# A two-layer hybrid SSM backbone on one core: layer 0's normed input leaves PSUM on two engines, S5 tables are computed without a wait for memory, and the order of background steps changes

## The chip, the cores and the metric

The kernel runs on one core of a Trainium2 chip. Its engines are TensorE (PE, matrix products into PSUM), VectorE (DVE), ScalarE (ACT), GpSimd (POOL) and SyncE (SP, which here only issues transfers). Each engine runs its own list of instructions in order, and instructions of different engines are tied by semaphores. The metric is the device time of one execution in microseconds (us); lower is better.

## The reference, cut to what matters

Two layers work on 512 tokens, 256 of context and 256 latent, of 1024 values each. A conditioning vector gives six modulation rows per layer through a matrix-vector product (`w_mod`); rows 0 and 1 shift and scale the normed input of the mixer, row 2 gates the mixer's result, rows 3 to 5 do the same around the feed-forward block.

```python
def _modulate(h, shift, scale):
    return h * (1.0 + scale) + shift
...
    for l in range(DEPTH):
        m_l = jnp.split((s_c @ w_mod[l] + b_mod[l])[:, None, :], N_MOD, axis=-1)
        m_c = jnp.split(s_cc @ w_mod[l] + b_mod[l], N_MOD, axis=-1)
        p_l = _split_in(_modulate(_rms_norm(x, norm_mix[l]), m_l[0], m_l[1]) @ w_in[l])
        p_c = _split_in(_modulate(_rms_norm(ctx, norm_mix[l]), m_c[0], m_c[1]) @ w_in[l])
        ...  # S5, retention and gated linear attention on columns of p_c and p_l
        x = x + m_l[2] * _merge_branches((s5_l, ret_l, gla_l), p_l[11:14], w_brs, w_out[l])
        x = x + m_l[5] * _swiglu(_modulate(_rms_norm(x, norm_ffn[l]), m_l[3], m_l[4]), w_ffn_in[l], w_ffn_out[l])
```

The S5 branch needs tables that hang on its parameters alone: powers and rotations of 64 complex states, made of exponentials, sines and cosines. They do not depend on the tokens.

## The kernel before, in words

**Products.** All large products are fp32 split in two rounded parts: an operand is hi + lo, and a product is three matmuls, hi·hi, hi·lo and lo·hi (`mm3`). SP loads a weight tile into a ring of three (`raw`), ACT rounds it (`hi`, line 228), DVE subtracts (`lo`, line 231; both in a ring of four). Tokens lie in the buffer `rb`, hi and lo beside each other, with the 1024 features on 8 blocks of 128 partitions.

**Order.** A list scheduler with a simulated timeline and priorities (`prio`) fixes, at build time, the order of each engine's instructions; on the chip each engine takes them strictly in that order. Memory in SBUF is handed out by two allocators, `arena` (20992 words per partition) and `zone` (5632 words). A new object takes the piece that was freed longest ago, and its first writer waits for whoever used that piece last. PSUM has rings of four banks (`mm`, accumulators), three (`mx`) and one (`sd`).

**The head of layer 0.** `layer` (line 1315 on) loads the tokens and scales them by their inverse norm (`xscale`, results `xs`). Then it goes over four chunks c of 256 features:

- `mod_chunk(c)` makes shift and scale of these features: two transfers of 1 MB (line 437), a matrix-vector product of 64 small matmuls and 8 for the bias, one row copy by ACT, one transpose, three small DVE steps into `mod`. In the page and the trace this is `b<-arena,sil`, `arena<-b 128x128` and `mod<-b`.
- `norm_chunk(c)` transposes the chunk, 8 blocks of 128 by 128 in two banks. DVE multiplies each bank by the scale (`arena<-b,mod` 128x512, line 231) and adds the shift (`arena<-arena,mod`), which gives one fp32 object of 1024 per partition (`h32`). ACT rounds all of it into `rb` hi (128x1024), DVE subtracts into `rb` lo (128x1024).
- `pack_mms(c)` runs 24 matmuls 128x512 into four accumulators, with weights from `pack_weights` (lines 540 and 541).

`pack_out` then empties the four accumulators, and `load_params2` transposes further parameters.

**S5 tables and asides.** `s5_tables` computes the tables in `zone`; `hold`, an object of 1536 words in `zone`, is given back only after it. Other work that hangs on no token is kept as a list of generators, the asides; later stages call `tick`, which runs the next step of the first. They are the two S5 rotations (`s5_rot`), the S5 preparations (`s5_prep`) and the modulation rows that the head does not make (`mod_vec`, rows 2 to 5 of layer 0 and 0 to 5 of layer 1). Rows listed in `ON_VECTOR`, among them 4 and 5 of layer 0, are accumulated by DVE: per 128 rows of weights one step of 128x1024 for each of two accumulators (`zone<-wm,sil,zone`), 16 in all; rows 2 to 5 of layer 1 have one accumulator, 8 steps. The bias row of each is loaded by SP into `zone`.

**Around the asides** stand layer 0's mixers, gates (up to about 405 us), merge (the branch projections and their sum, about 405 to 455 us), the output product and the feed-forward block (FFN).

## Time and profile before

| | |
|---|---|
| three runs | 1400.59, 1400.7 and 1404.64 us, median 1400.7 us |
| profiled execution, first to last instruction (span) | 1395.2 us; its own time is not given beside it, and the median is 5.5 us above the span |
| mean granted TensorE clock | 0.985 |
| busy: PE, DVE, ACT, POOL | 1344.3, 908.3, 577.4 and 75.6 us |
| moved by DMA | 257.33 MB, 184 GB/s on average |

A busy time is the sum over an engine's instructions. A wait is the time in which an engine has nothing to run, put down to the instruction or transfer whose semaphore came last. A window gives for a stretch of the span each engine's busy time, the granted TensorE clock as a share of full speed, and what the transfers moved. The list of the head's instructions by time runs from 0 to about 65 us, where the last matmul of chunk 3 ends.

### The profile page before, as it was taken

What the parts mean: (1) busy time and instruction counts of PE and PEld (TensorE: products, weight loads), DVE (VectorE), ACT (ScalarE), POOL (GpSimd) and SP (SyncE); (2) the same over time, 40 slices, a digit from 0 to 9 for tenths busy, and PEclk for the clock granted to TensorE, in tenths of its full rate; (3) what the DMA queues carried; (4) which work ended last, traced back from release to release, by engine and by line L of the source; (5) the groups of instructions that cost most, each with busy time, mean ns of one, the idle gap of its engine ahead of it and who ended that gap; (6) DMA issues with size and microseconds to landing.
All of it is one profiled execution on the core that took longest, in us unless ns stands there. A gap on an engine that the chain in (4) does not pass through costs nothing.

```text
span 1395.2 us, 22070 instructions
## 1 busy us (share of the span) xinstructions
PE 1344.3 (96%) x8559; PEld 1140.9 (82%) x8559; DVE 908.3 (65%) x1423; ACT 577.4 (41%) x930; POOL 75.6 (5%) x111
## 2 busy tenths in 40 slices
PE   4899999999999999999999999999999999899996
PEld 3788888787777778788777778888999997899985
DVE  4579782838889564545554788645876778555555
ACT  3367352323432343222222447545564364444442
POOL 3310000001100020000000000100000100000000
PEclk9999999999999999999999999999999999899999
DMA  9744465668968554733344786644766866466662
GB/s 305 213 115 119 139 200 182 213 197 271 303 210 280 173 165 125 234 109 121 106 129 129 279 310 193 181 112 111 199 170 163 238 191 215 117 198 197 184 192 91
DMA packets 258817, 257.33 MB, mean 184 GB/s; under 512 B 27200, under 2 KB 219244, under 8 KB 258200
## 3 DMA queue, kind: packets, MB, share of 16 engines
q1 hardware_dynamic: 244360, 230.41, 55.0%
q10 hardware_dynamic: 11392, 20.39, 4.2%
q0 software_dynamic: 2960, 5.12, 1.4%
q8 instruction: 67, 1.10, 0.3%
q14 instruction: 38, 0.31, 0.1%
HBM read 231.79 MB, written 24.08 MB: 183 GB/s over the span
## 4 chain that ended last, share of the span: by engine, by line
PE 85%; DMA 6%; DVE 5%; issue 2%; ACT 2%; SPq 1%; DVEq 0%; POOL 0%; POOLq 0%; ACTq 0%
PE b L243 83%; PE b L253 2%; DVE arena L231 2%; DVE lo L231 1%; DMA wm<-in_w_mod_dram 1%; DMA arena<-in_w_mod_dram 1%; DMA raw<-in_w_in_dram 1%; DMA raw<-in_w_ffn_out_dram 1%; DMA arena<-wb 1%; ACT arena L228 1%; DMA arena<-in_ctx_dram 1%; ACT hi L228 1%; DVE rb L231 0%; DVE zone L234 0%; DMA raw<-in_w_ffn_in_dram 0%
## 5 line engine op out<-in xcount | busy, mean ns | idle before, releaser
L243 PE MATMUL b<-rb,hi 128*128 128x256 f32 (+1 forms) x2784 | 695.1, 340 | 6.2 <-ACT rb L228 4.7
L243 PEld LDWEIGHTS b<-rb,hi 128*128 128x128 f32 x2784 | 481.9, 193 | 70.1 <-issue 11.1
L228 ACT ACTIVATE hi<-raw 128x1024 fp32r<-128x1024 f32 (+3 forms) x298 | 293.0, 989 | 458.0 <-PE b L243 350.4
L243 PE MATMUL b<-rb,lo 128*128 128x256 f32 (+1 forms) x1392 | 471.3, 339 | 0.0
L231 DVE TENSOR_TENSOR lo<-raw,hi 128x1024 fp32r<-128x1024 f32 (+3 forms) x298 | 338.3, 1140 | 199.4 <-ACT hi L228 190.4
L243 PE MATMUL b<-hi,rb 128*128 128x512 f32 (+2 forms) x1168 | 346.2, 374 | 3.9 <-DVE arena L570 3.3
L243 PEld LDWEIGHTS b<-rb,lo 128*128 128x128 f32 x1392 | 268.7, 193 | 31.7 <-issue 5.4
L243 PEld LDWEIGHTS b<-hi,rb 128*128 128x128 f32 x1168 | 216.5, 188 | 39.2 <-issue 4.1
L243 PE MATMUL b<-lo,rb 128*128 128x512 f32 (+2 forms) x584 | 217.0, 373 | 0.0
L243 PE MATMUL b<-arena 64*64 64x96 f32 (+8 forms) x1104 | 132.8, 288 | 0.3 <-DVE arena L231 0.3
L243 PEld LDWEIGHTS b<-lo,rb 128*128 128x128 f32 x584 | 109.8, 188 | 15.3 <-issue 1.3
L243 PEld LDWEIGHTS b<-arena 128*128 128x128 f32 (+4 forms) x1104 | 102.6, 167 | 20.2 <-issue 7.1
L231 DVE TENSOR_TENSOR arena<-arena 128x512 f32<-128x512 f32 (+5 forms) x174 | 105.6, 622 | 17.7 <-ACT arena L228 16.7
L234 DVE SCALAR_TENSOR_TENSOR arena<-arena,b 128x512 f32<-128x512 f32 (+1 forms) x136 | 74.2, 552 | 51.0 <-PE b L243 50.6
L228 ACT ACTIVATE arena<-b 128x512 f32<-128x512 f32 (+6 forms) x138 | 66.5, 486 | 73.9 <-PE b L243 59.6
L228 ACT ACTIVATE rb<-arena 128x256 fp32r<-128x256 f32 (+3 forms) x133 | 60.8, 473 | 84.3 <-PE b L243 57.2
L231 DVE TENSOR_TENSOR zone<-zone 128x512 f32<-128x512 f32 (+6 forms) x127 | 73.7, 604 | 28.6 <-DMA wb<-zone 17.4
L234 DVE SCALAR_TENSOR_TENSOR zone<-wm,sil,zone 128x1024 f32<-128x1024 f32 x56 | 70.9, 1283 | 18.7 <-DMA wm<-in_w_mod_dram 18.3
L231 DVE TENSOR_TENSOR rb<-arena,rb 128x256 fp32r<-128x256 f32 (+2 forms) x106 | 54.4, 522 | 21.1 <-ACT rb L228 20.7
L228 ACT ACTIVATE arena<-arena 128x512 f32<-128x512 f32 (+3 forms) x61 | 36.5, 601 | 30.6 <-DVE arena L231 19.9
L253 PE MATMUL b<-cst,arena 128*128 128x128 f32 (+1 forms) x178 | 30.4, 290 | 18.8 <-DMA arena<-in_norm_mix_dram 9.6
L491 POOL TENSOR_TENSOR st<-st,mh 128x1 f32<-128x1 f32 x16 | 11.6, 727 | 658.9 <-DVE st L240 657.9
(137 smaller groups left out, 660.4 us busy)
## 6 DMA issues: line engine op xcount, KB each, us to landing
raw<-in_w_ffn_in_dram SPq DMA_DIRECT2D x88, 512.0 KB
wm<-in_w_mod_dram SPq DMA_DIRECT2D x80, 512.0 KB
raw<-in_w_ffn_out_dram SPq DMA_DIRECT2D x66, 512.0 KB
raw<-in_w_in_dram SPq DMA_DIRECT2D x48, 512.0 KB
raw<-in_w_in_dram SPq DMA_DIRECT2D x48, 384.0 KB
raw<-in_w_out_dram SPq DMA_DIRECT2D x16, 512.0 KB
arena<-in_w_mod_dram SPq DMA_DIRECT2D x7, 1024.0 KB
wb<-zone ACTq DMA_DIRECT2D x8, 512.0 KB
```

Of the source, the lines that this page charges most:

```text
L228: self.S.activation(out, in_, f, bias=bias, scale=scale)
L231: self.V.tensor_tensor(out=out, in0=a, in1=b, op=op)
L234: self.V.scalar_tensor_tensor(out=out, in0=a, scalar=s, in1=b, op0=op0, op1=op1)
L243: self.P.matmul(out, l, r, start=start, stop=stop, **k)
L253: self.P.transpose(out, in_, self.ident[:k, :k])
L491: self.G.tensor_tensor(out=st[:, 3:4], in0=st[:, 2:3], in1=self.mh[:, 0:1], op=ALU.pow)
```

## The change

`norm_chunk` works on half a bank at a time: ACT computes scale times value plus shift straight from PSUM and writes the rounded result into `rb` (four ACT steps of 128x256 per chunk in place of one of 128x1024). DVE computes the same from PSUM in full precision with one two-operation step (`tensor_scalar`, four of 128x256 per chunk in place of two products and two sums of 128x512), and subtracts per bank (two of 128x512 in place of one of 128x1024). The transposes in a bank are ordered by feature block. In the kernel after, an ACT step and a DVE step that read the same bank are ordered one behind the other by semaphores.

All weights of `mod_chunk` and all four `xs` lie in `arena`, `hold` is gone, so `zone` is empty when `s5_tables` is built. The rotation of layer 0 follows at once and is no aside; the rotation of layer 1 stands in the list right ahead of layer 1's preparation. The list of modulation rows was 2 3 4 5 of layer 0, then 2 1 0 3, layer 1's preparation, 4 5 of layer 1. It is now 2 3 4 of layer 0, 1 0 of layer 1, 5 of layer 0, 2 3 of layer 1, rotation and preparation, 4 5 of layer 1.

```diff
 def asides(self, names):
     for c in names:
         if c == "p":
+            self.aside("rot", self.s5_rot(1, self.s5d[1]))
             self.aside("prep1", self.s5_prep(1, self.s5d[1]))
...
     for m in (1, 0):
-        ws[m] = (self.zone if c == 3 and m else self.arena).new(KD, 256)
+        ws[m] = self.new(KD, 256)
...
 def norm_chunk(self, c, xs):
     ks = slice(2 * c, 2 * c + 2)
-    h32 = self.new(4, 2, 128)
+    sh, sc = self.mod[:, 0, 0], self.mod[:, 0, 1]
     for s in range(2):
+        h32 = self.new(2, 2, 128)
         b = self.bank()
-        for t in range(2):
-            for k in range(2):
-                o = 128 * (2 * t + k)
+        rows = slice(1 + 2 * s, 3 + 2 * s)
+        for k in range(2):
+            for t in range(2):
+                o = 128 * (2 * k + t)
                 self.transpose(b[:, o:o + 128], xs[2 * s + t].ap[:, 128 * (2 * c + k):128 * (2 * c + k) + 128])
-        hv = h32.ap[:, 2 * s:2 * s + 2]
-        bc = lambda a: a[:, None, ks, s:s + 1].to_broadcast([128, 2, 2, 128])
-        self.tt(hv, b.rearrange("p (t k c) -> p t k c", t=2, k=2), bc(self.mod[:, 0, 1]), ALU.mult)
-        self.tt(hv, hv, bc(self.mod[:, 0, 0]), ALU.add)
-    self.act(self.rb[:, 1:5, 0, ks], h32.ap, AF.Copy)
-    self.tt(self.rb[:, 1:5, 1, ks], h32.ap, self.rb[:, 1:5, 0, ks].bitcast(F32), ALU.subtract)
-    self.drop(h32)
+        for k in range(2):
+            kk = 2 * c + k
+            src = b[:, 256 * k:256 * k + 256].rearrange("p (t c) -> p t c", t=2)
+            self.act(self.rb[:, rows, 0, kk], src, AF.Identity, scale=sc[:, kk, s:s + 1], bias=sh[:, kk, s:s + 1])
+            self.ts(h32.ap[:, :, k], src, sc[:, kk, s:s + 1], sh[:, kk, s:s + 1], ALU.mult, ALU.add)
+        self.tt(self.rb[:, rows, 1, ks], h32.ap, self.rb[:, rows, 0, ks].bitcast(F32), ALU.subtract)
+        self.drop(h32)
...
-            xs = [self.xscale(x.ap, self.arena if t > 1 else self.zone) for t, x in enumerate(xin)]
-            hold = self.zone.new(1536)
+            xs = [self.xscale(x.ap) for x in xin]
...
         with self.inside(self.zone):
             self.s5_tables()
-        self.drop(hold)
-        for x in range(2):
-            self.aside("rot", self.s5_rot(x, self.s5d[x]))
+            for _ in self.s5_rot(0, self.s5d[0]):
+                pass
         self.aside("prep0", self.s5_prep(0, self.s5d[0]))
-        self.asides("2345cbadpef")
+        self.asides("234ba5cdpef")
```

Three places show how the instructions stand. The first is DVE around the normed chunk 1, before. `mod` is written from the bank of the transposed rows, the banks b_294 and b_301 hold the transposed tokens, and the two `lo` rows split a weight tile of the pack product:

```order
L234 SCALAR_TENSOR_TENSOR mod<-b_289,par 128x2 x2
L458 COPY mod<-b_289 128x4
L231 TENSOR_TENSOR arena<-b_294,mod 128x512
L231 TENSOR_TENSOR arena<-b_301,mod 128x512
L231 TENSOR_TENSOR arena<-arena,mod 128x512 x2
L231 TENSOR_TENSOR rb<-arena,rb 128x4x256
L231 TENSOR_TENSOR lo_408<-raw_404,hi_407 128x16x48
```

And after, DVE at the same chunk, whose first bank is b_298; the `zone` rows belong to the S5 tables and to layer 0's rotation:

```order
L234 SCALAR_TENSOR_TENSOR mod<-b_293,par 128x2 x2
L459 COPY mod<-b_293 128x4
L231 TENSOR_TENSOR zone<-zone,cst 128x512
L240 TENSOR_SCALAR zone<-zone 128x512
L231 TENSOR_TENSOR zone<-zone 128x576
...
L238 TENSOR_SCALAR zone<-zone 128x512
L231 TENSOR_TENSOR zone<-zone 128x32 x2
L231 TENSOR_TENSOR lo_681<-raw_677,hi_680 128x832
L316 CAST msk<-arena 128x256
...
L240 TENSOR_SCALAR arena<-b_298,mod 128x2x128
```

Steps of the S5 tables, which stood behind the whole head before, now stand between `mod` and the first read of the chunk's bank.

The second place is PE at chunk 3, before: bias and weights of chunk 3's matrix-vector product stand ahead, chunk 3's transposes (b_477, b_482, b_489) come next, and then the first products of chunk 2 (weights hi_407):

```order
L253 MATMUL b_477<-cst,arena 128x128
L253 MATMUL b_482<-cst,zone 128x128 x4
L253 MATMUL b_489<-cst,arena 128x128 x4
L243 MATMUL b_151<-rb,hi_407 128x512
L243 MATMUL b_152<-rb,hi_407 128x512
```

And after, PE at the same transposes (b_489, b_494, b_504); hi_419 and lo_420 are the weights of chunk 2, hi_517 those of chunk 3:

```order
L243 MATMUL b_154<-rb,hi_419 128x512 x2
L243 MATMUL b_154<-rb,lo_420 128x512
L253 MATMUL b_489<-cst,arena 128x128
L253 MATMUL b_494<-cst,arena 128x128 x4
L253 MATMUL b_504<-cst,arena 128x128 x4
L253 MATMUL b_580<-cst,arena 128x128
L253 MATMUL b_754<-cst,zone 128x128
L243 MATMUL b_151<-rb,hi_517 128x512
```

Chunk 3's transposes moved from ahead of chunk 2's 24 products to behind them.

The third place is SP's list of transfers in the head, before, from the first weights of `mod_chunk` on (raw_216, raw_310 and raw_404 are weights of the pack product):

```order
L437 DMA arena<-in_w_mod_dram 128x8x256 x2
L540 DMA raw_216<-in_w_in_dram 128x2x384
L541 DMA raw_216<-in_w_in_dram 128x2x128
L437 DMA arena<-in_w_mod_dram 128x8x256 x2
L540 DMA raw_310<-in_w_in_dram 128x2x384
L541 DMA raw_310<-in_w_in_dram 128x2x128
```

And after, SP from the same place:

```order
L438 DMA arena<-in_w_mod_dram 128x8x256 x2
L543 DMA raw_220<-in_w_in_dram 128x2x384
L544 DMA raw_220<-in_w_in_dram 128x2x128
L438 DMA arena<-in_w_mod_dram 128x8x256
L543 DMA raw_318<-in_w_in_dram 128x2x384
L544 DMA raw_318<-in_w_in_dram 128x2x128
L543 DMA raw_416<-in_w_in_dram 128x2x384
L544 DMA raw_416<-in_w_in_dram 128x2x128
L438 DMA arena<-in_w_mod_dram 128x8x256 x2
```

The second half of chunk 1's `mod_chunk` weights now stands behind two tiles of `w_in`.

## Rows read from the trace of the kernel before

**Rows 1.** Page, busy time, share of span, instructions; then granted clock in 40 slices.
```profile
PE 1344.3 (96%) x8559; PEld 1140.9 (82%) x8559; DVE 908.3 (65%) x1423; ACT 577.4 (41%) x930; POOL 75.6 (5%) x111
...
PEclk9999999999999999999999999999999999899999
```

**Rows 2.** Page, chain that ended last, shares of the span by engine.
```profile
PE 85%; DMA 6%; DVE 5%; issue 2%; ACT 2%; SPq 1%; DVEq 0%; POOL 0%; POOLq 0%; ACTq 0%
```

**Rows 3.** PE's waits over the span: releaser, us in total, times, longest.
```profile
PE b L243 <- DMA arena<-in_w_mod_dram: 8.0, 2, 6.3
...
PE b L243 <- ACT rb L228: 4.7, 3, 2.2
PE b L243 <- DVE arena L570: 3.3, 2, 1.8
PE b L253 <- ACT arena L228: 2.2, 3, 1.4
PE b L243 <- DVE rb L231: 1.5, 2, 1.1
...
PE b L243 <- DMA zone<-in_b_mod_dram: 1.3, 1, 1.3
```

**Rows 4.** Windows: length, PE, PEld, DVE, ACT, POOL busy, clock, DMA, GB/s.
```profile
20.00:30.00 10.00, 7.97 (x126) 6.56 (x117) 6.65 (x13) 3.27 (x7) 5.27 (x10) 0.83 1.10 348
30.00:40.00 10.00, 10.00 (x83) 7.55 (x82) 5.51 (x11) 2.21 (x3) 6.87 (x13) 1.00 1.11 340
40.00:50.00 10.00, 8.24 (x128) 6.42 (x126) 4.31 (x10) 3.38 (x6) 3.60 (x7) 1.00 0.83 241
50.00:60.00 10.00, 8.26 (x39) 6.53 (x40) 7.21 (x18) 3.25 (x4) 4.74 (x10) 1.00 0.72 207
410.00:420.00 10.00, 9.67 (x41) 7.52 (x42) 8.11 (x12) 1.40 (x2) 0.00 (x0) 0.83 0.62 189
420.00:455.00 35.00, 35.00 (x176) 27.16 (x174) 33.56 (x50) 8.20 (x15) 1.72 (x2) 1.00 0.88 278
```

**Rows 5.** DVE in order of time, chunks 2 and 3: start, duration, [idle before].
```profile
51.77 1.29 DVE L231 TENSOR_TENSOR arena<-b,mod 128x512 f32<-128x512 f32 x2
52.98 1.22 DVE L231 TENSOR_TENSOR rb<-arena,rb 128x1024 fp32r<-128x1024 f32 x1
...
56.72 1.23 DVE L231 TENSOR_TENSOR rb<-arena,rb 128x1024 fp32r<-128x1024 f32 x1 [0.83 <-ACT rb L228]
```

**Rows 6.** DVE's groups by shape, 0 to 130 us: count, busy, mean ns.
```profile
L234 DVE SCALAR_TENSOR_TENSOR zone<-zone 128x512 f32<-128x512 f32 x12 | 8.1, 688 | 0.0
...
L234 DVE SCALAR_TENSOR_TENSOR zone<-zone 128x576 f32<-128x576 f32 x3 | 2.3, 755 | 0.0
L231 DVE TENSOR_TENSOR zone<-zone 128x32 f32<-128x32 f32 x13 | 2.0, 186 | 0.0
L238 DVE TENSOR_SCALAR zone<-zone 128x512 f32<-128x512 f32 x4 | 1.7, 424 | 0.0
...
L240 DVE TENSOR_SCALAR arena<-b,par 128x512 f32<-128x512 f32 x2 | 1.5, 748 | 3.1 <-ACT arena L228 3.1
```

**Rows 7.** Instructions on the tile `mod`: duration min/median/max in ns, first and last start.
```profile
L240 DVE TENSOR_SCALAR arena<-b,mod x40: 400/404/411, 500.7 to 1194.7; 128x128 f32<-128x128 f32 x40
```

**Rows 8.** PE in order of time: start, duration, count, [idle before and releaser].
```profile
25.93 3.23 PE L243 MATMUL b<-arena,sil 128*32 128x128 f32 x64 [1.64 <-DMA arena<-in_w_mod_dram]
...
58.96 1.29 PE L243 MATMUL b<-rb,hi 128*128 128x512 f32 x5
...
64.17 0.39 PE L243 MATMUL b<-rb,lo 128*128 128x512 f32 x1
...
108.68 0.44 PE L243 MATMUL b<-hi,rb 128*128 128x384 f32 x1 [1.79 <-DVE arena L570]
...
410.33 0.63 PE L243 MATMUL b<-zone,one 1*32 1x256 f32 x8 [1.34 <-DMA zone<-in_b_mod_dram]
```

**Rows 9.** Page, one step of an aside accumulated by DVE: count, busy, mean ns.
```profile
L234 DVE SCALAR_TENSOR_TENSOR zone<-wm,sil,zone 128x1024 f32<-128x1024 f32 x56 | 70.9, 1283 | 18.7 <-DMA wm<-in_w_mod_dram 18.3
```

## The prediction

> **What bounds the kernel now.** I read the page's busy times first: PE works 1344.3 of 1395.2 us and DVE 908.3 [rows 1], and the chain that ended last runs on PE for 85% of the span [rows 2]. So the time is PE's work plus its gaps, about 51 us. The change leaves the matmuls as they are. What it can move is the gaps, and the stretches in which PE was granted its lower clock. I therefore read PE's waits next. Those the change touches are: weights of the matrix-vector products 8.0, `rb` hi 4.7 in all (3 waits, not all in the head), the pack copies of line 570 3.3 in two, ACT's row copies 2.2, `rb` lo 1.5, and a bias row 1.3 [rows 3]. Then the windows of the head: from 20 to 60 us DVE is busy 6.65 + 5.51 + 4.31 + 7.21 = 23.7 of 40 us, ACT 12.1 [rows 4]. In the first half the transfers run at 340 to 348 GB/s with the DMA engines full (share 1.10 and 1.11) [rows 4]. So early on the head waits for data, and between 40 and 60 for the chain product, row copy, transposes, modulation, split. The split of chunk 2 ends at 52.98 + 1.22 = 54.2 and that of chunk 3 at 56.72 + 1.23 = 57.95 [rows 5]; the last product of chunk 3 ends at about 64.5 [rows 8].
>
> The sum below is made against the span of 1395.2 us. The median of the runs is 5.5 us above it, and I add that to the result. About 0.3%, or 4.2 us, is what a measurement of this kernel can tell from no change.
>
> **The normed chunk.** Before, DVE did per chunk four steps of 128x512, two pairs of 1.29 each, and one subtraction of 1.22 [rows 5]: 3.8 us. After, it does four steps of 128x256 from PSUM. The trace has 128x128 from PSUM at 0.404 [rows 7] and 128x512 at 0.748 [rows 6], so about 0.52 each lies between them, bounds 0.40 and 0.75. Two subtractions of 128x512, at the 0.688 of the same shape [rows 6], come on top: 2.1 + 1.4 = 3.5 us. DVE's load is unchanged within 0.3 us a chunk. What gets shorter is the chain, since ACT need not wait for all of DVE's sums. In each bank, however, ACT and DVE take turns, four steps one behind another.
>
> The row on this is that shape's price alone, 0.404 [rows 7]; it can't show what sharing a bank costs. The Trainium skill, in "PSUM — Partial Sum Buffer", section "PSUM bank collisions raise a hardware error", states that two engines may not touch one bank and quadrant at a time, reads against reads included. By that rule the two readers do not overlap within a bank, which speaks against the change; by an overlap they would save some 1 us a chunk. No trace of before shows it, and the sum does without it.
>
> **The S5 steps in DVE's queue.** This is the term that I think decides. With `zone` empty, the scheduler has moved the S5 tables and layer 0's rotation from behind the head into it; the first order piece shows them standing between chunk 1's `mod` and the first read of its bank. Up to chunk 2's last split I count seven two-input steps of 576 at 0.755, three one-input steps of 576 (about 0.46, the 512 form's 0.424 scaled), eight two-input steps of 512 at 0.688, six one-input steps of 512 at 0.424 and about 23 small ones at 0.186 [rows 6]: 5.3 + 1.4 + 5.5 + 2.5 + 4.3 = 19 us. Steps that follow each other overlap by nearly 0.1 us, as the 1.29 for two of 0.688 shows [rows 5, 6], so 16 to 19 us of queue time.
>
> From 20 to 60 us DVE was idle 40 - 23.7 = 16.3 us [rows 4]. The added steps fill that. An engine that takes its list in order then has no room left, and any wait for data that remains is paid in full. Replaying the list by these durations from about 25 us, when chunk 0's first tile split can run, I get 57 us for chunk 2's split (54.2 before), with 54 if nothing ever waits and 60 if every turn in the banks does. Everything behind a late `mod` slips with it: the three `mx` banks turn over only when DVE has read them, so chunk 2's product starts later too.
>
> **Chunk 3's place on PE.** Before, its transposes stood ahead of chunk 2's products, so its modulation ran under 24 matmuls, 5.4 us at a pitch of (1.29 - 0.39) / 4 = 0.225, from a run of five and a single one [rows 8]. Now the transposes stand behind those 24. From chunk 2's split at 57 I count 5.4 us of products, 0.9 of transposes and about 4 us for four turns in a bank (2.2) and two subtractions with their waits. That puts chunk 3's split at 67.4 (57.95 before), and the 20 products that need it end at 72, against 64.5 before. **Head: +7.5 us**, bounds +4.5 (split of chunk 2 at 54) and +11.
>
> **SP's list.** Half of chunk 1's weights now stands behind two tiles of `w_in`, together 1.05 MB, 3 us at 345 GB/s [rows 4]. Its product, which started at 25.93 as the weights landed [rows 8], starts at about 28.5. This is inside the +7.5, since DVE is the later of the two.
>
> **Gaps that go.** The wait of 1.79 at 108.68 is for DVE's copies [rows 8], which stood in a queue full of S5 steps; with these done earlier I take -1, bounds -1.8 and 0. The bias row at 410.33 cost 1.34 [rows 8] because its place in `zone` came free late. PE then ran at 0.83 of its clock from 410 to 420 [rows 4], that is 3.4 us at 1.2 GHz, or 1.7 us lost. The new list of asides loads that row earlier: -3, bounds -3 and 0.
>
> **Merge.** Row 5 of layer 0, with two accumulators, now falls partly into the merge: for five of its column blocks DVE has two steps of 128x1024 in place of one, each 1.28 and about 1.20 in a row [rows 9]. There DVE was busy 33.56 of 35 us and PE 35.00 [rows 4]. Five blocks at 1.2 are 6 us more, but the list around them has some 4 us less of other steps, and weights are split up to two tiles ahead. I take +1, bounds 0 and +4. In exchange the gates before it get lighter, which gains nothing where PE had no gap.
>
> **Clock.** PE had 0.83 in three stretches shown, 20 to 30, 40 to 50 and 410 to 420 [rows 4]; each cost 1.7 us. A barer head can add one: +1.4, bounds 0 and +3.4. The end of the program, layer 1's last mixers and its FFN, stands in the same order; 0. GpSimd's small loads for the parameters start later than before but land ahead of their transposes by my replay; 0, bounds 0 and +3.
>
> Sum: 7.5 - 1 - 3 + 1 + 1.4 = +5.9, a span of 1401.1 and a time of **1407 us**.
>
> **Rivals.** *Nothing to measure.* DVE's idle time was spread as short waits for transfers until 45 us. If the S5 steps sit in exactly those, the chunks slip by no more than chunk 3's bare chain, +4, less the 4 of the gaps that go: 1400 to 1402. For it speaks that 16.3 us idle against 16 is a near match; against it that the steps stand ahead of `mod`'s readers, not behind.
>
> *Faster.* The chain from PSUM to `rb` is what the head's gaps hang on. If it shortens and DVE keeps up, the waits for `rb` hi and lo and for ACT's row copies in the head go: of 4.7, 2.2 and 1.5 [rows 3] about 3.5 us lie between 40 and 60, where PE had 8.24 and 8.26 of 10. With 1.8 at 108.68, 3 at 410 and the S5 steps gone from a later DVE queue, that is -8 and +1 for the merge: 1394. It decides from the point at which chunk 2's split ends before 52 us. Against it stands the load of DVE.
>
> *Far slower.* DVE bounds the merge (+4), the parameters land late (+3) and the clock falls once more (+2): 1413 to 1416.
>
> *The change does not do what it says.* Were the S5 steps still waiting for memory, the head would gain or lose only by the chain; since the built order shows them moved, I give this no share.
>
> **How the numbers follow.** Forecast, head +4.5 to +11: 1403 to 1411, chance 0.55. Nothing to measure 0.22, faster 0.12, far slower 0.11. Leaving out most of the faster case and the top of the far slower one gives 1398 to 1414. Slower by over 0.3% means over 1404.9: most of the forecast and all of far slower, 0.60. Same: 0.22 and the low end of the forecast, 0.28. Faster: 0.12.
>
> **What would show it.** The windows of 20 to 60 us should show DVE at 36 us or more of 40, and PE with about 7 us less than before. Chunk 2's and chunk 3's last splits should end near 57 and 67, the last product of chunk 3 near 72. The gaps at 108.68 and 410.33 should be smaller or gone, the second with its low clock. I am wrong if DVE still has idle time of 6 us or more in that stretch and chunk 3's split ends before 60, or if the merge's PE falls below 33 of 35 us.

## The result, and the profile after

The changed kernel takes 1445.8 us (median of 6 runs, 1439.3 to 1456.0), the kernel before 1400.8 in the same session: a ratio of 1.0325 [1.0294, 1.0357], so 45 us slower. The forecast was 1407 us with a range up to 1414. The direction was right, the size by far not. The profiled execution is the fastest of the six; it has a span of 1437.5 us, 42.3 above that of before.

The page of the kernel after, with busy times by engine and the granted clock in 40 slices of 36 us (they answer to [rows 1]):

```profile
span 1437.5 us, 22081 instructions
...
PE 1358.5 (95%) x8559; PEld 1145.4 (80%) x8559; DVE 909.4 (63%) x1427; ACT 580.3 (40%) x942; POOL 79.5 (6%) x111
...
PEclk9899999999999998999999999999999999899999
...
PE 75%; DVE 11%; DMA 8%; issue 3%; ACT 2%; SPq 1%; POOL 0%; DVEq 0%; ACTq 0%; POOLq 0%
```

DVE is as busy as before, 909.4 us against 908.3. PE holds 75% of the chain where it had 85% [rows 2]; the rest went to DVE and to transfers. The clock digit is 8 in the second, the sixteenth and one late slice. PE's waits, in us in total, times, longest (before: [rows 3]):

```profile
PE b L253 <- DVE arena L238: 7.1, 3, 5.9
...
PE b L253 <- ACT arena L228: 5.0, 3, 3.7
PE b L253 <- DVE arena L240: 4.8, 3, 2.6
```

Lines 238 and 240 are DVE steps on normed rows, ACT's line 228 with `arena` here is their modulation, and PE's line 253 is the transposes of such rows. The longest of these waits, 5.9 us, lies behind 600 us, and the kernel before has it there too (6.1). New are those between 460 and 600 us: 1.2 us for line 238, 3.9 for line 240 and 3.7 for ACT, where the kernel before has none. How the loss is spread is told by windows over the whole span. Columns are length, busy time of PE, PEld, DVE, ACT and POOL, granted clock, DMA share, GB/s. Before:

```profile
0.00:80.00 80.00, 57.18 (x505) 48.13 (x506) 44.32 (x110) 27.09 (x51) 24.18 (x49) 0.98 0.80 239
80.00:460.00 380.00, 376.55 (x2397) 301.59 (x2396) 286.60 (x447) 156.48 (x244) 24.39 (x26) 1.00 0.67 206
460.00:520.00 60.00, 60.00 (x347) 45.23 (x347) 34.11 (x55) 22.59 (x45) 8.51 (x12) 1.00 0.51 160
520.00:600.00 80.00, 80.00 (x445) 66.77 (x445) 39.28 (x47) 22.72 (x33) 0.00 (x0) 1.00 0.58 178
```

and after:

```profile
0.00:80.00 80.00, 51.29 (x448) 40.56 (x449) 52.22 (x146) 33.65 (x66) 31.34 (x57) 0.91 0.79 236
80.00:460.00 380.00, 372.38 (x2430) 291.20 (x2429) 232.93 (x351) 139.68 (x219) 16.00 (x12) 1.00 0.64 193
460.00:520.00 60.00, 54.55 (x237) 39.64 (x236) 53.71 (x71) 14.86 (x26) 0.00 (x0) 0.94 0.71 236
520.00:600.00 80.00, 69.13 (x403) 59.34 (x402) 52.51 (x90) 35.42 (x62) 14.28 (x18) 0.91 0.46 133
```

A window's length less PE's busy time is what PE idled; its length times (1 - clock) is what the lower clock cost. In the head PE idles 28.7 us in place of 22.8, and loses 7 to the clock in place of 2. From 460 to 600 us, where before it idled not at all and ran at full clock, it now idles 5.5 + 10.9 = 16.3 us and loses about 10 more.

Counted over the whole trace (idle times over 0.25 us summed, and half of the time at 1.2 GHz), the difference closes:

| stretch | idle | clock | sum |
|---|---|---|---|
| 0 to 80 us | +5.4 | +5.1 | +10.5 |
| 80 to 460 | +4.0 | -1.7 | +2.3 |
| 460 to 600 | +16.1 | +10.2 | **+26.3** |
| behind 600 | +1.7 | -0.1 | +1.6 |
| whole trace | +27.2 | +13.5 | +40.7 of 42.3 |

What is left once idle time and clock loss are taken off the span is 1323.9 us before and 1325.4 after. So the matmuls cost the same, as the prediction said, and nearly all of the loss is waiting and clock. The two columns overlap a little, since PE idled during part of the time at 1.2 GHz: with that time counted once, as idle, the clock's part is +7.0 from 460 to 600 and +10.7 in all, and the sum is +38.0 of 42.3.

**The head.** PE of the kernel after, in order of time around chunk 3 (start, duration, instructions, [idle before and releaser]; before: [rows 8]):

```profile
70.54 0.50 PE L243 MATMUL b<-rb,hi 128*128 128x512 f32 x1 [2.44 <-DVE rb L231]
...
74.97 0.39 PE L243 MATMUL b<-rb,lo 128*128 128x512 f32 x1
```

and DVE, its last splits of chunk 2 (56.25) and chunk 3 (69.21), and the turns before them:

```profile
54.90 0.53 DVE L240 TENSOR_SCALAR arena<-b,mod 128x256 f32<-128x256 f32 x1
55.36 0.41 DVE L240 TENSOR_SCALAR zone<-zone 128x512 f32<-128x512 f32 x1
55.69 0.53 DVE L240 TENSOR_SCALAR arena<-b,mod 128x256 f32<-128x256 f32 x1
...
56.25 1.28 DVE L231 TENSOR_TENSOR rb<-arena,rb 128x512 fp32r<-128x512 f32 x2
...
69.21 1.28 DVE L231 TENSOR_TENSOR rb<-arena,rb 128x512 fp32r<-128x512 f32 x2
```

S5 steps (`zone`) do stand between the modulation steps. Chunk 2's split ends at 57.5 (57 was predicted), chunk 3's at 70.5 (67.4), the last product at about 75.4 (72).

**The new place.** PE of the kernel after where layer 0's output product ends (538.3) and the FFN begins:

```profile
538.31 0.63 PE L243 MATMUL b<-zone,one 1*32 1x256 f32 x8
539.96 1.09 PE L253 MATMUL b<-cst,arena 128*128 128x128 f32 x8 [1.01 <-DVE arena L238]
...
546.67 0.94 PE L253 MATMUL b<-cst,arena 128*128 128x128 f32 x4 [3.69 <-ACT arena L228]
...
549.56 1.11 PE L253 MATMUL b<-cst,arena 128*128 128x128 f32 x4 [1.26 <-DVE arena L240]
553.32 1.12 PE L253 MATMUL b<-cst,arena 128*128 128x128 f32 x4 [2.65 <-DVE arena L240]
...
557.61 0.58 PE L243 MATMUL b<-rb,hi 128*128 128x256 f32 x1 [2.10 <-DVE rb L231]
557.98 0.42 PE L243 MATMUL b<-rb,lo 128*128 128x256 f32 x1
```

From the end of the output product to the first FFN product with the `lo` tokens (558.0) it takes 19.6 us, and PE idles 1.01 + 3.69 + 1.26 + 2.65 + 2.10 = 10.7 us of them. The same place of the kernel before, where it takes 4.7 us without an idle one:

```profile
506.58 0.63 PE L243 MATMUL b<-zone,one 1*32 1x256 f32 x8
507.14 0.63 PE L243 MATMUL b<-wm,sil 128*32 128x256 f32 x6
507.71 1.09 PE L253 MATMUL b<-cst,arena 128*128 128x128 f32 x8
508.73 0.62 PE L243 MATMUL b<-wm,sil 128*32 128x256 f32 x2
...
511.36 0.28 PE L243 MATMUL b<-rb,lo 128*128 128x256 f32 x1
```

There the matmuls `wm,sil` of a modulation row (row 1 or 0 of layer 1, which PE accumulates) fill the time between the norm's transposes. In the kernel after none is left. The tile `wm` on PE: count, duration min/median/max in ns, first and last start, before

```profile
L243 PE MATMUL b<-wm,sil x256: 378/380/404, 245.1 to 565.8; 128*32 128x256 f32 x128
```

and after

```profile
L243 PE MATMUL b<-wm,sil x256: 379/379/404, 236.0 to 427.1; 128*32 128x256 f32 x128
```

In exchange DVE has its accumulations here. DVE of the kernel after, shortly ahead of the handover:

```profile
521.53 1.28 DVE L234 SCALAR_TENSOR_TENSOR zone<-wm,sil,zone 128x1024 f32<-128x1024 f32 x1
522.73 0.68 DVE L231 TENSOR_TENSOR arena<-arena 128x512 f32<-128x512 f32 x1
...
529.59 1.28 DVE L234 SCALAR_TENSOR_TENSOR zone<-wm,sil,zone 128x1024 f32<-128x1024 f32 x1 [2.33 <-DMA wm<-in_w_mod_dram]
...
532.85 0.68 DVE L231 TENSOR_TENSOR arena<-b,arena 128x512 f32<-128x512 f32 x1
```

These steps stand in DVE's list among the residual sums (`arena<-arena`, `arena<-b,arena`) and may wait there for their weights, 2.33 us in the last of them. Behind the sum at 522.73 the next one starts at 532.85, and the row norm and its transposes come after the sums. From 428 to 530 us there are 32 such steps; before, the stretch 460 to 520 had none.

Two more things lengthen the handover here. The change also puts layer 1's rotation behind these rows, and with it a table load of ACT (1.28 us) ahead of the norm's squares, for which DVE then waits. And ACT's modulation steps, for which PE waits the 3.69 us, stand behind the rounding of a weight tile; its transfer was issued at 541.06, when the ring of weights came free behind DVE's late split.

```profile
535.24 1.28 ACT L228 ACT_TABLE_LOAD   x1
...
538.43 0.21 DVE L240 TENSOR_SCALAR st<-st 128x1 f32<-128x1 f32 x1 [1.91 <-ACT arena L491]
...
544.83 1.06 ACT L228 ACTIVATE hi<-raw 128x1024 fp32r<-128x1024 f32 x1 [2.25 <-DMA raw<-in_w_ffn_in_dram]
```

### The profile page after: what moved, and what is told of

It reads as the page before. It is cut to its first block, busy times and chain, and to the rows that moved or that the text cites. A ratio compares the mean times of both kernels' runs of the same rounds, so it can differ in the third digit from the quotient of the medians.

```text
span 1437.5 us, 22081 instructions
## 1 busy us (share of the span) xinstructions
PE 1358.5 (95%) x8559; PEld 1145.4 (80%) x8559; DVE 909.4 (63%) x1427; ACT 580.3 (40%) x942; POOL 79.5 (6%) x111
## 4 chain that ended last, share of the span: by engine, by line
PE 75%; DVE 11%; DMA 8%; issue 3%; ACT 2%; SPq 1%; POOL 0%; DVEq 0%; ACTq 0%; POOLq 0%
PE b L243 73%; DMA wm<-in_w_mod_dram 4%; DVE zone L234 2%; DVE arena L231 2%; DVE lo L231 2%; DMA raw<-in_w_in_dram 2%; DVE arena L234 1%; PE b L253 1%; DVE zone L231 1%; DMA arena<-wc 1%; ACT arena L228 1%; DVE arena L240 1%; DVE rb L231 0%; ACT hi L228 0%; DMA arena<-ydr 0%
## 5 line engine op out<-in xcount | busy, mean ns | idle before, releaser
L243 PEld LDWEIGHTS b<-lo,rb 128*128 128x128 f32 x584 | 110.4, 189 | 17.5 <-DVE lo L231 2.6
L228 ACT ACTIVATE rb<-arena 128x256 fp32r<-128x256 f32 (+3 forms) x129 | 56.8, 455 | 95.1 <-PE b L243 69.2
L231 DVE TENSOR_TENSOR rb<-arena,rb 128x256 fp32r<-128x256 f32 (+1 forms) x110 | 55.0, 508 | 30.2 <-ACT rb L228 30.1
L253 PE MATMUL b<-cst,arena 128*128 128x128 f32 (+1 forms) x194 | 34.4, 306 | 28.2 <-DMA arena<-in_norm_mix_dram 8.6
L228 ACT ACTIVATE arena<-arena 128x512 f32<-128x512 f32 (+3 forms) x61 | 36.4, 600 | 46.4 <-DVE arena L231 26.3
L253 PEld LDWEIGHTS b<-cst,arena 128*128 128x128 f32 (+1 forms) x194 | 25.1, 154 | 35.6 <-issue 11.4
```

What stands on the lines that cost most here:

```text
L228: self.S.activation(out, in_, f, bias=bias, scale=scale)
L231: self.V.tensor_tensor(out=out, in0=a, in1=b, op=op)
L243: self.P.matmul(out, l, r, start=start, stop=stop, **k)
L253: self.P.transpose(out, in_, self.ident[:k, :k])
```

## The experiments

A place that returns below is the **handover**: from the end of layer 0's output product to the first `lo` product of the FFN, given with its length and with what PE idles in it.

### One part of the change at a time

**The normed chunk alone.** The `norm_chunk` of the change put into the kernel before:

```diff
-            self.tt(hv, b.rearrange("p (t k c) -> p t k c", t=2, k=2), bc(self.mod[:, 0, 1]), ALU.mult)
-            self.tt(hv, hv, bc(self.mod[:, 0, 0]), ALU.add)
...
+                self.act(self.rb[:, rows, 0, kk], src, AF.Identity, scale=sc[:, kk, s:s + 1], bias=sh[:, kk, s:s + 1])
+                self.ts(h32.ap[:, :, k], src, sc[:, kk, s:s + 1], sh[:, kk, s:s + 1], ALU.mult, ALU.add)
```

> The kernel before with the new normed chunk alone; memory, S5 tables and the order of asides are those of before. Theory 1 (DVE's queue: the S5 steps cost the head, the DVE steps of the moved modulation row cost the merge and the output product): nothing of that is here, so 1397 to 1402 us, the wait for rb hi in the head shorter, head end within 3 us of before's 64.5. Rival 2 (ACT and DVE taking turns at one PSUM bank is what costs the head): 1405 to 1412 us, with waits for rb lo in the head of 4 us or more.

Measured 1417.4 us, 1.0140 [1.0105, 1.0176]. The head is no later: its last products begin at 63.5 us (64.2 before). Taking turns in a bank costs nothing that reaches PE here. The loss is 360 us further on, in the layer's later stages. DVE of this kernel:

```profile
424.00 1.28 DVE L235 SCALAR_TENSOR_TENSOR zone<-wm,sil,zone 128x1024 f32<-128x1024 f32 x1 [1.26 <-DMA wm<-in_w_mod_dram]
425.21 3.69 DVE L232 TENSOR_TENSOR rb<-arena,rb 128x512 fp32r<-128x512 f32 x6
```

and PE, which waits for that split:

```profile
426.55 0.79 PE L244 MATMUL b<-rb,hi 128*128 128x512 f32 x1 [5.94 <-DVE rb L232]
```

The edit touches nothing there. The scheduler made a new list for the whole program, and in this one a split stands behind accumulations that wait for weights. From 80 to 460 us this kernel idles 10.8 us more than the one before and loses 8.5 us more to the clock, which is nearly its whole loss. The expected time fell, and so did the rival.

**The S5 tables at once, alone** (the memory places and the early rotation):

```diff
-            hold = self.zone.new(1536)
...
-            for x in range(2):
-                self.aside("rot", self.s5_rot(x, self.s5d[x]))
+                for _ in self.s5_rot(0, self.s5d[0]):
+                    pass
+            self.aside("rot", self.s5_rot(1, self.s5d[1]))
```

> The kernel before with the memory edit alone: zone empty, S5 tables and layer 0's rotation computed without a wait for memory, old normed chunk, old order of modulation rows, layer 1's rotation the first aside. Theory 1: the S5 steps stand in DVE's queue ahead of the chunks, so the head ends 8 to 12 us later than before's 64.5 and the time is 1406 to 1413 us, with no gaps of PE between 440 and 560 us beyond before's. Rival 2: within 3 us of before, 1398 to 1404 us. Rival 3 (the three edits only cost together): within 3 us of before as well.

Measured 1426.0, 1.0194 [1.0144, 1.0244]. The last products of the head begin at 80.7 us, 16.5 later than before. The window of the head:

```profile
0.00:80.00 80.00, 46.27 (x422) 35.28 (x423) 53.72 (x139) 31.29 (x57) 32.38 (x61) 0.89 0.83 247
```

DVE is busy 9.4 us more than before here and PE 10.9 less. From 460 to 600 PE idles nowhere. So this part makes the head's loss, and not the later one. The head's idle time and clock are 17.7 us of this run's loss; another 12 us went to a lower clock between 80 and 460 us, where PE idles 2.3 us less than before.

**The order of the background rows, alone:**

```diff
-            self.asides("2345cbadpef")
+            self.asides("234ba5cdpef")
```

(the rotation of layer 1 with it, as in the change).

> The kernel before with the order of the asides alone: modulation rows 2 3 4 of layer 0, 1 0 of layer 1, 5 of layer 0, 2 3 of layer 1, then layer 1's rotation and preparation. Theory 1: the head is that of before within 1 us, and merge, output product and the norm behind it get 18 us of PE gaps and up to 10 us of lower clock, as in the kernel after: 1422 to 1432 us. Rival 3 (the asides cost only because the head has moved everything later): 1398 to 1404 us.

Measured 1431.6, 1.0245 [1.0205, 1.0286], the costliest part by itself. PE idles 12.8 us between 460 and 600 us, and the handover has 5.7 us idle. The head changed too (last products at 72.7), which no theory had: the transposes of chunk 3 stand behind chunk 2's products in this list also.

**Normed chunk and tables, with the old order of the rows:**

```diff
-            self.asides("234ba5cdpef")
+            self.asides("2345cbadpef")
```

(against the kernel after, with the rotation first as before).

> The kernel after with the old order of the asides (layer 1's rotation as the first aside). Theory 1: the head loss of the kernel after is all here and the later one is gone: head end 72 to 77 us, 1408 to 1414 us. Rival 3 (the loss comes with the asides alone): 1399 to 1404 us. If the new normed chunk saves what theory 1 grants it, this run is 0 to 3 us below the run with the memory edit alone.

Measured 1416.7, 1.0133 [1.0101, 1.0165]. The head is late, its last products begin at 79.4 us, but between 460 and 600 us nothing is lost: PE is busy 140.00 of 140 us at a clock of 1.00.

**Normed chunk and row order, with the S5 tables waiting as before** (`hold` and the old places back in the kernel after).

> The kernel after with the S5 tables and rotation waiting for memory as before: new normed chunk and new order of asides. In its list the S5 steps stand behind chunk 3's split. Theory 1: the head ends by 67 us (75.7 in the kernel after), the loss around merge, output product and norm stays at 20 us or more, 1424 to 1434 us. If the head still ends past 72 us, the S5 steps are not what made the head late.

Measured 1437.9, 1.0265 [1.0232, 1.0299]. The head ends at 66.7, near that of before, and the later stretch is as in the kernel after: PE is busy 122.52 of 140 us at 0.90 of its clock.

These five divide the loss by place: the early tables go with the late head, the row order with 460 to 600. But the times don't add up. Alone the three parts lose 20, 27 and 34 us by their ratios, 81 in all; together they lose 45. The tables' own cost hangs on the rest: with the normed chunk in place they add -1 us (1.0140 to 1.0133), with normed chunk and row order +8 (1.0265 to 1.0325).

### What a change costs that changes nothing

Two edits of the kernel before that leave its work alone. One swaps two transfers that are issued in a row, the other takes and drops 512 words of memory:

```diff
-        for m in (1, 0):
+        for m in (0, 1):
```

```diff
+                self.drop(self.arena.new(512))
```

> The kernel before with one neutral edit: the two 1 MB loads of a chunk's modulation weights are issued shift first instead of scale first. Same bytes, same instructions, but the scheduler makes a new plan, and about as many rows of the engines' lists move (1122) as with the new normed chunk alone (1184). Theory 4 (each edit costs mainly because the plan is made anew and comes out worse than before's): 1412 to 1430 us, with low-clock stretches or gaps of PE between 130 and 460 us that before has not. Theory 1 (each edit costs by what it does): 1396 to 1404 us.

> The kernel before with another neutral edit: an object of 512 words in arena is taken and given back ahead of the head, unused, so that all later objects lie elsewhere and the plan is made anew (1020 rows move). Theory 4: 1412 to 1430 us, with losses between 130 and 460 us. Theory 1: 1396 to 1404 us.

Measured over 10 runs each: 1407.6, 1.0051 [1.0031, 1.0071], and 1408.3, 1.0047 [1.0022, 1.0073]. They moved 1122 and 1020 rows of the planned lists; the new `norm_chunk` moves 1184. So a mere new draw of the plan costs about 7 us in these two, as much as my whole forecast of a loss. It can cost more: the normed chunk alone lost 20 us, 360 us away from the place that it edits. A part's own worth can't be read from the time of one kernel. In neither of the two does PE idle between 460 and 600 us; but their heads are later, with the last products at 70.0 and 67.7 us (64.2 before).

### What makes the loss between 460 and 600 us

**Rows (0,5) and (1,2) accumulated by PE** in the kernel after:

```diff
-ON_VECTOR = ((0, 4), (0, 5), (1, 2), (1, 3), (1, 4), (1, 5))
+ON_VECTOR = ((0, 4), (1, 3), (1, 4), (1, 5))
```

> The kernel after, with two modulation rows (5 of layer 0, 2 of layer 1) multiplied by PE instead of accumulated by DVE; the head keeps its order. 24 DVE steps of 128x1024 leave the stretch from 400 to 530 us, and PE gets 64 small matmuls of 256 columns, some 7 us. Theory 1: the gaps of 18 us and the low clock worth 10 us between 430 and 560 us go for the most part: 1418 to 1428 us. Theory 4 (a plan made anew is worse anywhere): gaps of that size show up elsewhere and the time stays above 1435 us.

Measured 1437.9, 1.0264 [1.0221, 1.0307]. PE now has matmuls `wm,sil` up to 539.1; from 460 to 520 it idles nowhere, and the first handover takes 3.4 us with none idle. Behind that the filling is used up, and 6.1 us are idle from 552 to 561, where six accumulations stand on DVE. PE's added work, 128 small matmuls of some 11 us by my estimate, may eat the rest of the gain.

**The rotation of layer 1 first, as before,** in the kernel after.

```diff
-                self.aside("rot", self.s5_rot(1, self.s5d[1]))
...
+            self.aside("rot", self.s5_rot(1, self.s5d[1]))
```

> The kernel after with layer 1's rotation as the first aside again, the new order of modulation rows kept. Theory 5 (between 460 and 600 us PE lost the small matmuls of rows 1 and 0 of layer 1, which filled its waits there and kept it busy): the loss there stays, 10 us of gaps or more, and 1432 to 1445 us. Theory 6 (the rotation's steps on DVE and ACT in the norm's stage hold up the norm): gaps between 515 and 600 us fall below 4 us and the time to 1425 us or less.

Measured 1438.8, 1.0277 [1.0226, 1.0328], with 12.4 us idle from 460 to 600, 8.0 of them in the handover (18.7 us long). Shortly ahead of it DVE waits for the weights of its accumulations, up to 4.21 us. So the rotation's place is not the main cause; by this run it is worth 3 to 4 us of idle time.

**The old order of the rows** in the kernel after, the rest as it is:

```diff
-            self.asides("234ba5cdpef")
+            self.asides("2345cbadpef")
```

> The kernel after with the old order of modulation rows, layer 1's rotation still ahead of layer 1's preparation. Theory 5: rows 1 and 0 of layer 1 run on PE between 430 and 570 us again, gaps between 460 and 600 us fall below 3 us, 1412 to 1422 us. Theory 6: gaps of 8 us or more stay there and the time is over 1430 us.

Measured 1421.1, 1.0145 [1.0103, 1.0187], against 1.0325 for the kernel after: this one string is worth some 25 us. The last `wm,sil` on PE is at 529.9, and the first handover takes 3.4 us, none idle:

```profile
460.00:600.00 140.00, 135.17 (x747) 109.04 (x746) 86.00 (x128) 49.96 (x83) 7.55 (x12) 0.96 0.56 176
```

The 4.8 us idle that stay lie at 543 to 550, where the next tokens are normed and five accumulations stand on DVE.

So the order of the rows is the cause, and more than one pair of kernels shows it. By the ratios it costs 34 us in the kernel before and 17.5 with the normed chunk (both with the rotation moved), 20 with normed chunk and early tables, and 25 here. The five kernels that have the new order unaltered idle 12.4 to 18.8 us between 460 and 600 and 5.7 to 11.6 in the handover, with no `wm,sil` matmul in it. Of the kernels with the old order, six idle nowhere in that stretch, this one 4.8 us, and one that comes last below 1.5.

But it does two things at once there: it takes PE's small matmuls away, and it puts 32 steps on DVE. My theory was that the lost filling decides. Two kernels were to part the two.

**Fewer DVE steps.** In the kernel after, the accumulations of rows (0,5), (1,2) and (1,3) are left out but for the first of each; the weights are still loaded:

```diff
+                if k and (l, m) in ((0, 5), (1, 2), (1, 3)):
+                    continue
```

> The kernel after with most of the DVE accumulation of three modulation rows left out (5 of layer 0, 2 and 3 of layer 1: only the first 128 of 1024 rows of weights are multiplied; all weights are still loaded). 28 DVE steps of 128x1024 leave the stretch from 428 to 530 us, and no PE work is put there. If DVE's steps cause the gaps of 5.4 us between 460 and 520 us and the lost cover those of 10.7 us behind, the first fall below 1 us and 7 us or more of the second stay: 1430 to 1440 us. If DVE's steps cause both, both go: 1415 to 1425 us. If the lost cover causes both, both stay.

Measured 1433.4, 1.0207 [1.0162, 1.0251]. The two windows:

```profile
460.00:520.00 60.00, 51.52 (x212) 37.29 (x212) 36.64 (x63) 16.13 (x26) 8.21 (x14) 0.89 0.75 247
520.00:600.00 80.00, 76.83 (x452) 67.76 (x450) 55.56 (x87) 34.54 (x63) 2.61 (x4) 0.96 0.36 110
```

It came out the other way round: the second stretch was to keep its loss, and the handover shrank from 10.7 us idle to 3.0 and from 19.6 long to 8.1, with no `wm,sil` matmul to fill it. PE there:

```profile
548.93 0.66 PE L253 MATMUL b<-cst,zone 128*128 128x128 f32 x4 [1.63 <-ACT zone L228]
...
551.36 1.01 PE L243 MATMUL b<-rb,hi 128*128 128x256 f32 x3 [1.33 <-ACT rb L228]
```

So most of the handover's idle time, 7.7 of 10.7, went with the steps in DVE's list. Layer 1's rotation runs earlier in this list as well, but with the rotation alone moved 8.0 us stayed, so the steps are the larger part. The first stretch was to lose its gaps and got 8.5 us in place of 5.4. DVE there waits for a transfer:

```profile
508.91 0.69 DVE L231 TENSOR_TENSOR arena<-b,arena 128x512 f32<-128x512 f32 x1 [10.02 <-DMA arena<-gd]
```

`gd` holds the gate rows, which go through DRAM. SP issued this load at 493.76, behind the rows' weights in its list, where the kernel after issued it at 484.15; PE waited 3.98 us at 510.79 for the split behind it.

**More filling.** In the kernel after, rows 1 and 0 of layer 1 are multiplied a second time on PE behind row 2 (128 matmuls, 11 us of PE's time):

```diff
-            self.asides("234ba5cdpef")
+            self.asides("234ba5cbadpef")
```

> The kernel after with rows 1 and 0 of layer 1 multiplied a second time by PE, behind row 2: 128 small matmuls, 11 us of work that nothing needs, from 530 us on; DVE's list is that of the kernel after up to there. If the lost cover causes the gaps and the low clock between 520 and 600 us (10.7 us of gaps, 13.7 us at 1.2 GHz), they fall below 4 us and the time is that of after within 8 us in spite of 11 us more work; the gaps of 5.4 us between 460 and 520 us stay. If DVE's steps cause them, they stay at 8 us or more and the time is 1452 us or more.

Measured 1455.5, 1.0364 [1.0299, 1.0428]. The window and the handover:

```profile
520.00:600.00 80.00, 79.73 (x487) 66.38 (x486) 43.98 (x68) 31.65 (x57) 3.59 (x4) 1.00 0.44 132
```

```profile
545.59 0.64 PE L243 MATMUL b<-wm,sil 128*32 128x256 f32 x8
546.15 0.66 PE L253 MATMUL b<-cst,arena 128*128 128x128 f32 x4
```

The handover is that of the kernel before again (5.6 us, 0.3 idle), and the low clock is gone from the stretch. By the ratios the kernel is 5.5 us slower than the kernel after all the same: the doubled rows are some 11 us of work by my estimate, and a new loss came at 953 to 965 us. This kernel doesn't isolate the filling, since no accumulation stands on DVE in the 30 us ahead of the handover here either (seven in the kernel after), nor between 520 and 600 us (three). The two together read: idle time at the handover is 10.7 us with the steps on DVE and no filling, 3.0 without the steps, and 0.3 without the steps and with filling. Steps on DVE with filling, the fourth case, is not shown.

### The head, and the end of the program

**The S5 tables held back** in the kernel after until the first results of the pack product, its memory places kept:

```diff
-        nc.vector.memset(rows.ap, 0.0)
+        self.ts(rows.ap, gate.ap[:, :128], 0.0, None, ALU.mult)
...
-                self.s5_tables()
+                self.s5_tables(gqk[0])
```

> The kernel after with one dependency added: the first step of the S5 tables reads the first result of the pack (times zero), so no S5 step can stand ahead of the end of the head. Memory stays as in the kernel after. Theory 1 (S5 steps in DVE's queue made the head late): chunk 3's products end by 68 us (75.7 in the kernel after), and what is lost behind 460 us stays: 1430 to 1440 us. If the new memory places, and the transfers that wait for them, made the head late, chunk 3's products end past 72 us.

Measured 1428.4, 1.0209 [1.0175, 1.0242]. The head's last products begin at 71.1 us: between the two thresholds. The head of the kernel after slipped by 10.8 us (64.2 to 75.0); 4 of them are gone here, and with the old places too it is 66.7 (normed chunk and row order, above), another 4 less. The edits that change nothing moved the head by 3.5 and 5.8 us, so steps of 4 don't part the S5 steps from the places, the transfers that follow them, or the plan. What stands is the part as a whole: in the eight kernels with the tables early the last products begin at 74.7 to 80.8 us, in the eight others at 63.4 to 72.7. This run is also 0.6% below the one with normed chunk and row order, though its head is later and PE idles 18.8 us between 460 and 600; why, I have not found.

**Filling at the end of the kernel before.** Layer 1's last row goes from DVE to PE and into the stage ahead of the output product, where PE of the kernel before idles 8.1 us:

```diff
-ON_VECTOR = ((0, 4), (0, 5), (1, 2), (1, 3), (1, 4), (1, 5))
+ON_VECTOR = ((0, 4), (0, 5), (1, 2), (1, 3), (1, 4))
...
-            self.asides("2345cbadpef")
+            self.asides("2345cbadpe")
...
+        self.aside("mod15", self.mod_vec(1, 5, self.gd[1]))
```

> The kernel before with modulation row 5 of layer 1 multiplied by PE (64 small matmuls, about 5.5 us) in the output product of layer 1, in place of 8 DVE steps earlier; nothing ahead of 750 us moves. If theory 5 is right that such matmuls are worth most where PE waits, part of the 8.1 us of gaps and of the 13.7 us of low clock at 1183 to 1201 us goes: 1394 to 1400 us. If they only add work, 1403 to 1408 us.

Measured over 12 runs 1405.3, 1.0048 [1.0025, 1.0071]: no gain, and by the ratio 7 us more, as much as the two edits that change nothing. In the window aimed at, PE of this kernel has

```profile
1180.00:1205.00 25.00, 21.33 (x97) 16.54 (x96) 16.48 (x23) 11.93 (x19) 1.85 (x2) 0.98 0.61 185
```

where the kernel before has

```profile
1180.00:1205.00 25.00, 16.87 (x92) 15.28 (x91) 14.91 (x26) 11.26 (x21) 1.55 (x2) 0.73 0.32 90
```

The clock recovers and PE idles 3.7 us there in place of 8.1. That the new matmuls, 5.5 us by the expectation, cost what is given back is argued, not shown: the profiled execution was the slowest of the twelve and lost clock elsewhere. No version that I ran is faster than the kernel before.

## Why the prediction was wrong

- **The normed chunk: cost right.** DVE's step from PSUM takes 0.53 us (0.52 assumed), and by itself the new chunk leaves the head where it was. Its 20 us in that run came from a later place.
- **S5 steps in DVE's queue and chunk 3's place: size at the upper bound, cause in part shown.** The head lost 10.5 us, forecast 7.5, bound 11. Chunk 2's split came as computed; chunk 3's and the end of the head were 3 us later, with the clock at 0.83 over 20 to 60 us. DVE was busy 32.3 of those 40 us and not 36, so it was not full; and PE's busy time fell there by 2.0 us and not 7. The runs tie the late head to the early tables, but not to DVE's queue alone.
- **Gaps that go: right.** The waits at 108.68 and 410.33 [rows 8] are gone, PE runs 10.00 of 10 us from 410 to 420 at full clock. But 80 to 460 as a whole did not gain: PE idles 4 us more in other places.
- **The step that failed is the one headed Merge**, with the clock's +1.4 behind it. It looked for the moved row in the merge alone, at +1 with 0 to +4. There PE kept 32.7 of 35 us (420 to 455), just below the 33 that I had named as a sign of being wrong, but the loss lay behind it. I counted what the new order puts on DVE there, and neither followed the DVE steps beyond it (32 of them up to 530 us, through the output product and into the norm) nor asked what the rows that moved ahead of them had done where they stood: 1 and 0 of layer 1 were PE's filling up to 565.8 us. Both ends of the exchange hit the handover: DVE late with the norm, and PE with nothing else to do. The first is the larger (7.7 of 10.7 us idle go with DVE's steps); the second is shown only where those steps are gone (3.0 against 0.3). 26.3 us came from 460 to 600 us, with the clock's share of 10.2 in it.
- **The bound on the clock**, +3.4, came from three stretches of 10 us that lost 1.7 us each; the clock lost 13.5 more. In the kernel after 20.5 us of the stretch from 460 to 600 ran at 1.2 GHz, behind idle times and small transposes.
- **The rivals.** "Far slower" had the merge's DVE and the clock as its means, but with prices of 4 and 2 us. "Nothing to measure" and "Faster" fell with the head.
- **What no step named:** that a new plan by itself costs about 0.5%, or more, as the normed chunk alone shows. How much of the 42 us is of that kind is not shown.

What stays open: how much of the head is the S5 steps and how much memory places and plan; what filling alone would do for the handover while DVE's steps stay; and of the first stretch, 460 to 520 us, only that the old row order is free of its 5.4 us idle, since taking DVE's steps away moved the gap rather than removed it.

## What to carry to other kernels

Before background work is moved, look at what it does where it stands: small matmuls that look like a burden may be what PE runs while a norm or a split is under way, and the work that takes their place may stand in the queue that the norm needs. Follow a moved step to the end of its own run, not to the end of the stage it was moved into. And where a scheduler plans the whole program anew, time one or two edits that change nothing first: a difference of their size says nothing, and a larger one is safe only when several variants with the same part show it in the same place.

## What the runs showed of the hardware

The low clock was worth a quarter to a third of the loss, 10.7 to 13.5 of 42 us. Half of that came in one stretch of 13.7 us at 1.2 GHz, from 546.8 to 560.5 us, in the handover, where PE idled for 1 to 4 us at a time between transposes. The clock can also fall where PE shows next to no idle time. From 100 to 180 us the filled version of the kernel before has the same lists as that kernel, and its profiled execution shows

```profile
100.00:180.00 80.00, 78.20 (x562) 69.81 (x562) 61.99 (x108) 42.27 (x69) 3.46 (x6) 0.91 0.42 126
```

against

```profile
100.00:180.00 80.00, 78.21 (x612) 69.78 (x611) 65.94 (x115) 46.07 (x74) 4.62 (x7) 1.00 0.45 129
```

for the kernel before: PE is as busy, at 0.91 of the clock in one and 1.00 in the other, and 562 matmuls are counted against 612. By the same matmul in both lists, the one execution is 0.8 us ahead at 100 us and 5.4 us behind from 180 us on: 6.2 us. So in the small matmuls of the mixers the clock differs between two executions of the same lists, and a difference there in one profile says nothing of the edit.

Two readers of one bank, DVE with 0.54 us a step and ACT with 0.56, one behind the other, cost the head nothing: with the normed chunk alone it ends at 63.5 us against 64.2. The Trainium skill, in "PSUM — Partial Sum Buffer", section "PSUM bank collisions raise a hardware error", forbids that two engines touch a bank and quadrant at once; the turns that the kernel's semaphores make of it showed no price in that run's head.
